# Two-block model on one core: norms by pairs of column blocks, a freed modulation unit, one odd query product among the heads, a joined operand in the first feed-forward

## The chip, the core and the metric

The kernel runs on one core of a Trainium2 chip. The metric is the device time of one execution in microseconds (us). The engines are TensorE (PE in the profile; PEld is its weight load), VectorE (DVE), ScalarE (ACT), GpSimd (POOL) and SyncE (SP), which issues the transfers.

## The reference

A sequence of 256 tokens with 1024 features passes two blocks. The first (linear attention, two softmax attentions, a mixture of 32 experts) fills the first 600 us and is not touched. The second has two layers, each modulated by a condition vector `c`:

```
for l in range(2):
    mod = silu(c) @ ada_w[l] + ada_b[l]          # six parts: shift, scale, gate, twice
    h = rms_norm(x, norm_mix[l]) * (1 + scale1) + shift1
    x = x + gate1 * (mixer[l](h) @ w_out[l])     # layer 0: "even", layer 1: "odd"
    h = rms_norm(x, norm_ffn[l]) * (1 + scale2) + shift2
    x = x + gate2 * ((silu(h @ wg[l]) * (h @ wu[l])) @ wd[l])   # hidden width 2816
```

The odd mixer is attention in a window of 128 tokens: 16 query heads of 64 columns, 4 key heads, a learned sink in the softmax, a bias that falls with distance.

## The kernel before

Everything is in fp32. A product with a weight is made of two parts of each operand: `wh`, the weight cast to fp32r (ScalarE, L344), and `wl`, the rest (VectorE, L346); likewise `xh` and `xl` for the activations (L412, L413). Three products are added up in PSUM: wh·xh, wh·xl, wl·xh. Tokens are two tiles `t` of 128.

Feed-forward: four chunks of hidden columns, two in each half, and behind a half the product with `wd` for it. The gate and up products of layer 0 (`dense_T`, L499 to L501) take the three parts as three passes of 256 columns. Those of layer 1 (`dense_T2`, L480, L481) keep xh and xl side by side in one tile `xx`, so that one pass of 512 columns does wh·xh and wh·xl into two halves of a PSUM bank and one of 256 does wl·xh; the two halves are then added (`ev_g2`, `ev_u2`) by a ScalarE copy and a VectorE add. In layer 0 VectorE also computes eight units of the modulation (L725, L729: one weight piece times a scalar, added up), whose sums over partitions TensorE makes in passes of one column (L747).

Norm: the residual is added in halves of 512 columns, each is squared and summed (`square`, L424), the reciprocal root is made on ScalarE (Ln, Exp; L122) and VectorE, and put on a diagonal (`diag`, L437). A product with `diag` transposes and scales a 128 by 128 block of x (L389: `pt`), and the evacuation applies gain and shift (`evT`, L408 on ScalarE, two of 16 on VectorE, L410) before it is split into xh and xl. Modulation units not on VectorE are eight TensorE passes (`pa`, L719), a copy (`part`, L731) and one or four passes (`pq`, L739) that add up the parts; `MOD_AT` says at which place how many are done: at "ffn0" and "ffn1" two, at "even" and "odd" one.

Odd mixer: after keys and values, `dense` makes the query product of 512 columns for heads 0 to 7 (q0) and 8 to 15 (q1). Each is followed by four blocks of four heads (`Heads`, run by `run_heads`): scores (`ps`, L593), bias and row maximum (L601), Exp (L122), division (L556, L560), transposition (`pT`, L638), product with v (`po`, L648), split into `yh`, `yl`. Blocks of the first token tile have 128 keys, those of the second 256. The order in a queue is chosen when the program is built, by when tiles become free; `after` puts one instruction behind another by hand. `hold` remembers the instructions that others are put behind.

Of the kernel before, what the change touches and what calls it, by code (L numbers as in the profile page):

```python
# [9 lines left out]
F32 = mybir.dt.float32  # L10
# [9 lines left out]
KT = 8  # L20
# [58 lines left out]
def block_kernel(ctx: ExitStack, tc: tile.TileContext, a, out, stop=None):  # L79
# [299 lines left out]
    def to_T(xh, xl, src, t, gain=None, shift=None, pool=None, blocks=(0, 1), tags="tbb", diag=None):  # L379
        last = None  # L380
        for b in blocks:
            turn[1] += 1
            pt = bank("pt", tags[turn[1] % len(tags)])
            for k in range(4):
                piece = src[:, (4 * b + k) * 128:(4 * b + k + 1) * 128]
                if diag is None:
                    PE.transpose(pt[:, 128 * k:128 * k + 128], piece, ident)
                else:
                    i = PE.matmul(pt[:, 128 * k:128 * k + 128], piece, diag, start=True, stop=True)  # L389
                    if k == 0 and hold["pt"]:  # L390
                        after(i, hold["pt"])
                    hold["pt"] = i.ins
# [3 lines left out]
            if gain is None:  # L396
                split(hv, lv, pv)
            else:
                tmp = pool.tile([128, 4, 128], F32, tag="sq", name="evT", bufs=2)
                if shift is None:  # L400
                    V.tensor_tensor(tmp, pv, gain(4 * b, 4)[:, :, None].to_broadcast([128, 4, 128]), ALU.mult)
                    S.copy(hv, tmp)
                    (G if b else V).tensor_sub(lv, tmp, hv)  # L403
                    continue
                g, sh = gain(4 * b, 4), shift(4 * b, 4)
                for k in range(4):
                    if b == 0 or k < 3:
                        i = S.activation(tmp[:, k], pv[:, k], AF.Identity, scale=g[:, k:k + 1], bias=sh[:, k:k + 1])  # L408
                    else:
                        V.tensor_scalar(tmp[:, k], pv[:, k], g[:, k:k + 1], sh[:, k:k + 1], op0=ALU.mult, op1=ALU.add)  # L410
                for h in (slice(0, 2), slice(2, 4)) if b == t == 0 else (slice(0, 4),):
                    V.tensor_copy(hv[:, h], tmp[:, h])  # L412
                    last = (V.tensor_sub(lv[:, h], tmp[:, h], hv[:, h]).ins, i.ins)  # L413
        return last
# [6 lines left out]
    def square(t, c, in_turn=True):  # L421
# [5 lines left out]
        if c:  # L427
            ms = small.tile([128, 1], F32, tag="ms", name="ms")
            V.tensor_tensor(ms, sq[:, t, 0:1], sq[:, t, 1:2], ALU.add)
            norm_parts[1 + t] = rsqrt(ms, 1)  # L430

    def norm_T(xh, xl, gain, shift, pool, place):

        hold["q"], hold["pt"] = [], None
# [3 lines left out]
        for b in range(2):  # L438
            for t in range(2):
                last = to_T(xh, xl, x[:, t], t, gain, shift, pool, blocks=(b,), diag=diag[t])  # L440
                if b == 0:
                    ev0 = last[::-1]

        hold["q"] = [(hold["exp"] if place == "even" else None, hold["diag"]), ev0, last[::-1], last[::-1]]
        hold["last"] = last
# [22 lines left out]
    def dense_T2(xx, name, c0, w, evac, tags):  # L468
# [16 lines left out]

    def dense_T(xh, xl, name, c0, w, evac):

        n = w // 128
        ps = [bank("pd", "d") for _ in range(0, n, 2)]
        for k0 in range(0, KT, 4):  # L490
            wt, = load((name, c0, k0))
            for h0 in (0, 2):
                wh, wl = split_w(wt[:, h0 * w:(h0 + 2) * w])
                for k in range(2):
                    kk = k0 + h0 + k
                    for i in range(n):
                        o = ps[i // 2][:, i % 2 * 256:i % 2 * 256 + 256]
# [1194 lines left out]
```

## Time and profile before

| what | us |
|---|---|
| median of 3 runs (1257.46 to 1259.83) | 1259.74 |
| profiled execution | 1257.98 |
| its span in the trace | 1256.1 |
| first feed-forward (759.88 to 954.36) | 194.48 |
| odd mixer (961.70 to 1058.13) | 96.43 |
| norm ahead of the odd mixer / of the second feed-forward | 7.34 / 10.96 |

The trace counts from the span's start, and 1.88 us of the profiled execution lie outside it. A stage is read as a window: its length, how long each engine was busy in it, and the clock that TensorE was granted.

### The profile page before, as it was taken

Reading aid. Unit: us, or ns where it says so; the run is one execution under the profiler, and the core shown is the slowest. Engines: PE = TensorE matmul, PEld = TensorE weight load, DVE = VectorE, ACT = ScalarE, POOL = GpSimd, SP = SyncE. Lnnn points to the kernel's source line nnn. Section 1 sums busy time; section 2 is a strip of 40 time slices with the busy share of each in tenths; the row PEclk is TensorE's granted clock in tenths of the full one; section 3 lists DMA queues with packets and bytes.
Section 4 is the critical chain, followed back from the end, with each engine's and each line's share of the span. In section 5 each row is a group of like instructions: output and inputs, shape, how many; then the busy total and the mean of one; then the engine's idle time right before and its main releaser. Section 6 shows DMA issues by size and latency. Waiting matters only on the chain.

```text
span 1256.1 us, 17061 instructions
## 1 busy us (share of the span) xinstructions
PE 1153.2 (92%) x6575; PEld 779.5 (62%) x6575; DVE 636.8 (51%) x1403; ACT 473.8 (38%) x999; POOL 17.0 (1%) x23
## 2 busy tenths in 40 slices
PE   8999999789697978787999899999999999999998
PEld 6786764244141414111777559989996766888886
DVE  7687511201010101010689759876856666766674
ACT  5567500000000000000665746443456566664562
POOL 1020000000000000000000000000000000000000
PEclk9999999999998989888999899999999999999999
DMA  9967899999999999999976279978767515656520
GB/s 343 346 210 292 299 389 420 421 420 421 421 421 420 421 421 421 421 421 414 383 287 203 103 246 327 346 255 294 278 213 247 172 34 184 219 188 215 164 72 33
DMA packets 111289, 370.61 MB, mean 295 GB/s; under 512 B 6051, under 2 KB 19174, under 8 KB 86886
## 3 DMA queue, kind: packets, MB, share of 16 engines
q1 hardware_dynamic: 111122, 369.46, 77.7%
q8 instruction: 52, 0.85, 0.3%
q14 instruction: 31, 0.25, 0.1%
q10 hardware_dynamic: 84, 0.04, 0.0%
HBM read 368.43 MB, written 1.05 MB: 294 GB/s over the span
## 4 chain that ended last, share of the span: by engine, by line
PE 58%; DMA 31%; DVE 6%; ACT 3%; issue 0%; SPq 0%; DVEq 0%; ACTq 0%
DMA w<-in_w_gate_dram 10%; DMA w<-in_w_down_dram 10%; DMA w<-in_w_up_dram 9%; PE pd L357 8%; PE pd L361 8%; PE pd L360 8%; PE pd L480 7%; PE pd L499 3%; PE pd L500 3%; PE pd L501 3%; PE pd L481 3%; PE pgx L1442 2%; PE ps L593 2%; DVE wl L346 1%; PE gt L1467 1%; PE pa L719 1%
## 5 line engine op out<-in xcount | busy, mean ns | idle before, releaser
L346 DVE TENSOR_TENSOR wl<-w,wh 128x1024 fp32r<-128x1024 f32 (+5 forms) x264 | 267.8, 1022 | 138.1 <-ACT wh L344 135.1
L344 ACT CAST wh<-w 128x1024 fp32r<-128x1024 f32 (+5 forms) x264 | 231.2, 886 | 221.1 <-PE pd L360 112.3
L1467 PE MATMUL up<-w,xg 128*32 128x512 f32 x512 | 97.4, 682 | 38.8 <-DMA w<-in_w_up_dram 38.8
L480 PE MATMUL pd<-xx,wh 128*128 128x512 f32 x352 | 121.0, 394 | 0.6 <-DVE xx L413 0.6
L1478 DVE TENSOR_TENSOR hm<-hm,up 128x512 f32<-128x512 f32 x8 | 5.5, 688 | 201.6 <-PE up L1467 201.6
L1467 PE MATMUL gt<-w,xg 128*32 128x512 f32 x512 | 87.5, 634 | 20.0 <-DMA w<-in_w_gate_dram 14.3
L1490 PE MATMUL py<-w,hT 128*32 128x512 f32 x512 | 94.2, 609 | 9.6 <-DVE hT L1483 5.5
L499 PE MATMUL pd<-xh,wh 128*128 128x256 f32 x352 | 99.5, 285 | 0.0
L500 PE MATMUL pd<-xl,wh 128*128 128x256 f32 x352 | 99.2, 283 | 0.2 <-DVE xl L413 0.2
L501 PE MATMUL pd<-xh,wl 128*128 128x256 f32 x352 | 98.6, 283 | 0.0
L481 PE MATMUL pd<-xx,wl 128*128 128x256 f32 x352 | 95.3, 278 | 0.0
L357 PE MATMUL pd<-wh,xh 128*128 128x512 f32 (+3 forms) x240 | 90.5, 380 | 0.6 <-ACT wh L344 0.3
L1467 PEld LDWEIGHTS up<-w,xg 128*32 128x32 f32 x512 | 21.6, 121 | 109.1 <-DMA w<-in_w_up_dram 70.4
L360 PE MATMUL pd<-wh,xl 128*128 128x512 f32 (+3 forms) x240 | 88.1, 370 | 0.2 <-DVE xl L403 0.2
L361 PE MATMUL pd<-wl,xh 128*128 128x512 f32 (+3 forms) x240 | 83.7, 379 | 3.1 <-DVE wl L346 2.9
L480 PEld LDWEIGHTS pd<-xx,wh 128*128 128x128 f32 x352 | 65.7, 188 | 16.4 <-DVE xx L413 1.4
L1442 PEld LDWEIGHTS pgx<-hot,xn 128*128 128x128 f32 x256 | 62.4, 333 | 13.6 <-issue 11.6
L357 PE MATMUL pd<-wh,hidh 128*128 128x512 f32 x176 | 68.5, 389 | 0.0
L360 PE MATMUL pd<-wh,hidl 128*128 128x512 f32 x176 | 68.5, 389 | 0.0
L500 PEld LDWEIGHTS pd<-xl,wh 128*128 128x128 f32 x352 | 67.4, 192 | 0.5 <-DVE xl L413 0.4
L499 PEld LDWEIGHTS pd<-xh,wh 128*128 128x128 f32 x352 | 67.2, 192 | 0.8 <-DVE xh L412 0.7
L501 PEld LDWEIGHTS pd<-xh,wl 128*128 128x128 f32 x352 | 67.1, 192 | 0.0
(401 smaller groups left out, 1776.5 us busy)
## 6 DMA issues: line engine op xcount, KB each, us to landing
w<-in_w_gate_dram SPq DMA_DIRECT2D x64, 1024.0 KB, 19.8
w<-in_w_up_dram SPq DMA_DIRECT2D x64, 1024.0 KB, 19.8
w<-in_w_down_dram SPq DMA_DIRECT2D x62, 1024.0 KB, 19.8
w<-in_ada_w_dram SPq DMA_DIRECT2D x48, 1024.0 KB, 5.9
w<-in_ffn_down_dram SPq DMA_DIRECT2D x20, 1024.0 KB, 5.1
w<-in_ffn_gate_dram SPq DMA_DIRECT2D x16, 1024.0 KB, 5.1
w<-in_ffn_up_dram SPq DMA_DIRECT2D x16, 1024.0 KB, 6.2
w<-in_w_out_dram SPq DMA_DIRECT2D x12, 1024.0 KB, 6.4
```

What stands on the lines that cost most here:

```text
L344: i = S.copy(wh[:, :n], src)
L346: j = (G if share[0] and turn[0] % share[0] == 0 else V).tensor_sub(wl[:, :n], src, wh[:, :n])
L357: i = PE.matmul(o, xh, wh, start=start, stop=False)
L360: PE.matmul(o, xl, wh, start=False, stop=False)
L361: hold["pe"] = PE.matmul(o, xh, wl, start=False, stop=stop).ins
L480: PE.matmul(ps[i], wh[:, ws], xx[:, kk], start=kk == 0, stop=kk == KT - 1, skip_group_check=True)
L481: hold["pe"] = PE.matmul(ps[i][:, 0:256], wl[:, ws], xx[:, kk, 0], start=False, stop=kk == KT - 1, skip_group_check=True).ins
L499: PE.matmul(o, wh[:, ws], xh[:, kk], start=kk == 0 and i % 2 == 0, stop=False, skip_group_check=True)
L500: PE.matmul(o, wh[:, ws], xl[:, kk], start=False, stop=False, skip_group_check=True)
L501: hold["pe"] = PE.matmul(o, wl[:, ws], xh[:, kk], start=False, stop=kk == KT - 1, skip_group_check=True).ins
L1467: mm = PE.matmul(o[32 * j:32 * j + 32, :], xg[:, 4 * hk + k, 32 * j:32 * j + 32], ws[j][:, k * 512:(k + 1) * 512], start=hk == 0 and k == ...
L1490: PE.matmul(py[c][32 * j:32 * j + 32, :], hT[:, 2 * hk + k, 32 * j:32 * j + 32], ws[j][k][:, c * 512:(c + 1) * 512], start=hk == 0 and k = ...
```

## The change

- The first feed-forward uses `xx` as the second does; `dense_T` with three passes goes.
- The norm transposes in four PSUM tiles of two column blocks for all 256 tokens; ScalarE evacuates each 128 by 256 piece (8 in all). The passes of the last tile stand behind the first products. EPS is added to the first half's sum early, and Ln takes that sum as its bias, so no add stands between the last square and Ln.
- At "ffn0" and "ffn1" the first of the two units gets no order behind the mixer's last product, its `part` none behind the norm's Exp, and its `pq` none behind the transposes.
- q1 is made in four steps of 12 passes, which stand among the four head blocks of q0. The weight cast of steps 1 to 3 is put behind the last Exp of the softmax before (`hold["soft"]`).

```diff
@@ square
-        if c:
-            ms = small.tile([128, 1], F32, tag="ms", name="ms")
-            V.tensor_tensor(ms, sq[:, t, 0:1], sq[:, t, 1:2], ALU.add)
-            norm_parts[1 + t] = rsqrt(ms, 1)
...
+        elif c == 0:
+            V.tensor_scalar(sq[:, t, 0:1], sq[:, t, 0:1], EPS, None, op0=ALU.add)
+        else:
+            m0, m1 = sq[:, t, 0:1], sq[:, t, 1:2]
...
+            act(y, m1, AF.Ln, bias=m0)
+            hold["exp"] = act(y, y, AF.Exp, scale=-0.5).ins
@@ norm_T
-        for b in range(2):
-            for t in range(2):
-                last = to_T(xh, xl, x[:, t], t, gain, shift, pool, blocks=(b,), diag=diag[t])
...
+        for b, t in ((0, 0), (1, 0), (2, 0), (0, 1), (1, 1), (2, 1), (3, 0), (3, 1)):
+            if t == 0:
+                pts[b] = bank("pt", "tbbb"[b])
+            for k in range(2):
+                at_ = (2 * b + k) * 128
+                i = PE.matmul(pts[b][:, 256 * k + 128 * t:256 * k + 128 * t + 128], x[:, t, at_:at_ + 128], diag[t], start=True, stop=True)
...
+            for k in range(2):
+                i = S.activation(tmp[:, k], pts[b][:, 256 * k:256 * k + 256], AF.Identity, scale=g[:, k:k + 1], bias=sh[:, k:k + 1])
+            for h in (slice(0, 1), slice(1, 2)) if b == 0 else (slice(0, 2),):
...
+                V.tensor_copy(hv, tmp[:, h])
+                j = V.tensor_sub(lv, tmp[:, h], hv)
@@ modulation
+            free = norm and i < n - 1
+            begun.append(ada(*units.pop(0), TAG_AT(place), place in ON_DVE, norm and not free, None, False if free else norm or None))
+            if free or not norm and (len(begun) == 2 or place not in ON_DVE + ('odd1',)):
+                begun.pop(0)()
+        if norm:
+            modulated(hold["pt"])
@@ odd_mixer
+        dense(xh, xl, "odd", *C_ODD[1], ev_q(0))
+        q1 = dense_steps(xh, xl, "odd", *C_ODD[2], ev_q(4))
+
+        def step_q1(i):
+            if i:
+                hold["q"] = [hold["soft"]]
+            next(q1, None)
         for q in range(2):
-            dense(xh, xl, "odd", *C_ODD[1 + q], ev_q(4 * q))
...
+            if q:
+                run_heads(todo, lambda: early({k: (yh[:, k:k + 4], yl[:, k:k + 4]) for k in (0, 4)}))
+            else:
+                run_heads(todo, {i: lambda i=i: step_q1(i) for i in range(4)})
@@ feed-forward
-            if l:
-                xx = p3.tile([128, KT, 2, 256], F32R, tag="xx", name="xx")
-                xh, xl = xx[:, :, 0], xx[:, :, 1]
-            else:
-                xh = p3.tile([128, KT, 256], F32R, tag="xh", name="xh")
-                xl = p3.tile([128, KT, 256], F32R, tag="xl", name="xl")
+            xx = p3.tile([128, KT, 2, 256], F32R, tag="xx", name="xx")
+            xh, xl = xx[:, :, 0], xx[:, :, 1]
...
+                    dense_T(xx, f"ffg{l}", c0, w, ev_g, "dddt")
+                    modulated()
+                    dense_T(xx, f"ffu{l}", c0, w, ev_u, "ssbb")
```

TensorE's queue from the last out-projection product (`pd<-wl,yh`) through the norm ahead of the second feed-forward to its first products; a row with x8 is eight passes of the form. Before:

```order
L361 MATMUL pd<-wl,yh 128x512
L719 MATMUL pa<-w,condr 32x512 x8
L739 MATMUL pq<-part,pick_100 128x512
L719 MATMUL pa<-w,condr 32x512 x8
L389 MATMUL pt<-diag,x 128x128 x16
L739 MATMUL pq<-part,pick_100 128x512
L480 MATMUL pd<-xx,wh 128x512
L481 MATMUL pd<-xx,wl 128x256
```

After the change, behind six passes with the first tile's `diag` that follow the last product:

```order
L728 MATMUL pq<-part,pick_100 128x512
L708 MATMUL pa<-w,condr 32x512 x8
L438 MATMUL pt<-diag,x 128x128 x6
L490 MATMUL pd<-xx,wh 128x512
L491 MATMUL pd<-xx,wl 128x256
L490 MATMUL pd<-xx,wh 128x512
L491 MATMUL pd<-xx,wl 128x256
L490 MATMUL pd<-xx,wh 128x512
L491 MATMUL pd<-xx,wl 128x256
L490 MATMUL pd<-xx,wh 128x512
L491 MATMUL pd<-xx,wl 128x256
L438 MATMUL pt<-diag,x 128x128 x4
```

One unit's eight `pa` passes are gone from here (they stand among the out-projection's products now), the transposes are in pieces of six, six and four, and eight feed-forward products stand ahead of the last four.

TensorE's queue in the odd mixer: before, from the last of q1's products (`pd<-wh,xh` and its like) through the scores of q0's second block (128x128) to those of its wide blocks (128x256).

```order
L357 MATMUL pd<-wh,xh 128x512
L360 MATMUL pd<-wh,xl 128x512
L361 MATMUL pd<-wl,xh 128x512
L593 MATMUL ps<-kT,qT 128x128 x4
L638 MATMUL pT<-ident,sc 128x128 x4
L593 MATMUL ps<-kT,qT 128x256 x4
L648 MATMUL po<-pTs,v 64x128 x4
L357 MATMUL pd<-wh,yh 128x512
L593 MATMUL ps<-kT,qT 128x256 x4
L360 MATMUL pd<-wh,yl 128x512
```

After the change, from the last products of q1's first step, through the scores (`ps`) of the first three blocks, to the products of its second step (the x8 are the scores of two blocks):

```order
L360 MATMUL pd<-wh,xl 128x512
L361 MATMUL pd<-wl,xh 128x512
L556 MATMUL pt<-ident,qn 128x128 x4
L582 MATMUL ps<-kT,qT 128x128 x8
L582 MATMUL ps<-kT,qT 128x256 x4
L627 MATMUL pT<-ident,sc 128x128 x2
L582 MATMUL ps<-kT,qT 128x256 x2
L357 MATMUL pd<-wh,xh 128x512
L360 MATMUL pd<-wh,xl 128x512
L357 MATMUL pd<-wh,xh 128x512
L360 MATMUL pd<-wh,xl 128x512
L627 MATMUL pT<-ident,sc 128x128 x2
```

Before, half of q1's 48 passes stood ahead of the first score block and half between the first and the second, and only the out-projection's products (`pd<-wh,yh`) were left for the later blocks. Now the scores of the first two blocks and of one and a half wide ones follow each other, with one step of q1 ahead and the next behind.

## Rows read from the trace of the kernel before

**Rows 1.** The page: span, and the chain that ended last by engine.

```profile
span 1256.1 us, 17061 instructions
...
PE 58%; DMA 31%; DVE 6%; ACT 3%; issue 0%; SPq 0%; DVEq 0%; ACTq 0%
```

**Rows 2.** Windows by stage: length; PE, PEld, DVE, ACT, POOL busy; clock; DMA share, GB/s.

```profile
602.00:611.00 9.00, 7.43 (x58) 4.98 (x57) 6.25 (x20) 8.58 (x26) 0.00 (x0) 1.00 1.06 378
...
750.00:759.88 9.88, 9.15 (x69) 4.92 (x61) 6.35 (x20) 6.82 (x19) 0.00 (x0) 1.00 0.93 317
759.88:827.47 67.59, 67.37 (x561) 67.10 (x561) 58.46 (x81) 33.03 (x43) 0.00 (x0) 1.00 0.92 324
827.47:857.42 29.95, 29.95 (x135) 24.79 (x133) 26.88 (x36) 12.05 (x13) 0.00 (x0) 1.00 0.85 290
857.42:924.32 66.90, 66.90 (x562) 66.90 (x560) 46.49 (x60) 30.00 (x36) 0.00 (x0) 1.00 0.73 255
...
954.36:961.70 7.34, 6.32 (x52) 4.39 (x51) 5.93 (x21) 6.27 (x18) 0.55 (x2) 1.00 0.59 194
961.70:1058.13 96.43, 91.98 (x493) 66.42 (x491) 66.06 (x201) 62.94 (x172) 0.00 (x0) 0.98 0.40 134
1058.13:1069.09 10.96, 9.58 (x69) 5.07 (x68) 7.36 (x21) 7.58 (x22) 0.00 (x0) 1.00 1.03 373
1069.09:1130.38 61.29, 61.29 (x352) 53.55 (x353) 44.62 (x69) 39.67 (x72) 0.00 (x0) 1.00 0.61 199
...
1160.31:1221.44 61.13, 61.13 (x354) 53.43 (x352) 41.56 (x63) 36.18 (x65) 0.00 (x0) 1.00 0.38 125
```

**Rows 3.** Groups of VectorE, first gate and up half of layer 0 (759.88 to 827.47).

```profile
L729 DVE SCALAR_TENSOR_TENSOR part<-w,condr,part 128x512 f32<-128x512 f32 x28 | 20.0, 745 | 0.0
...
L725 DVE TENSOR_SCALAR part<-w,condr 128x512 f32<-128x512 f32 x4 | 1.8, 480 | 0.0
```

**Rows 4.** Groups of TensorE in the same window.

```profile
L747 PE MATMUL pq<-ones_r,part 128*128 128x1 f32 x32 | 3.8, 240 | 0.0
```

**Rows 5.** Timeline, norm ahead of the second feed-forward.

```profile
1057.34 0.40 PE L357 MATMUL pd<-wh,yh 128*128 128x512 f32 x1
...
1057.57 0.39 PE L360 MATMUL pd<-wh,yl 128*128 128x512 f32 x1
...
1058.13 1.93 PE L719 MATMUL pa<-w,condr 128*32 128x512 f32 x16
...
1060.14 0.59 ACT L731 COPY part<-pa 128x512 f32<-128x512 f32 x1 [0.60 <-DVE ms L429]
...
1061.06 0.61 ACT L424 ACTIVATE sqj<-x 128x512 f32<-128x512 f32 x1
```

**Rows 6.** Windows in the odd heads, columns as in rows 2.

```profile
1003.75:1037.29 33.54, 30.84 (x183) 21.59 (x183) 23.21 (x110) 23.30 (x83) 0.00 (x0) 0.95 0.10 32
1010.00:1015.00 5.00, 4.92 (x19) 3.70 (x17) 3.30 (x17) 3.35 (x16) 0.00 (x0) 0.66 0.44 169
```

**Rows 7.** Groups of ScalarE in the odd mixer.

```profile
L344 ACT CAST wh<-w 128x1024 fp32r<-128x1024 f32 x20 | 20.9, 1051 | 14.4 <-PE pd L360 13.1 <-issue 1.1
L122 ACT ACTIVATE sc<-sc,mx 128x256 f32<-128x256 f32 x16 | 7.9, 498 | 0.0
L122 ACT ACTIVATE sc<-sc,mx 128x128 f32<-128x128 f32 x16 | 6.2, 390 | 3.7 <-DVE mx L605 3.7
...
L556 ACT ACTIVATE sc<-sc,rc 128x256 f32<-128x256 f32 x8 | 3.6, 498 | 0.0
L554 ACT COPY pTs<-pT 128x512 f32<-128x512 f32 x6 | 3.5, 579 | 3.5 <-PE pT L638 3.4
```

**Rows 8.** Groups of TensorE in the odd heads (1003.75 to 1037.29).

```profile
L593 PE MATMUL ps<-kT,qT 64*128 64x256 f32 x32 | 8.6, 402 | 1.1 <-DVE mx L601 1.1
L638 PE MATMUL pT<-ident,sc 128*128 128x128 f32 x32 | 5.1, 283 | 0.0
...
L648 PE MATMUL po<-pTs,v 128*64 128x128 f32 x56 | 4.6, 285 | 0.0
```

More of the change, by code (lines that the diff above doesn't have):

```diff
@@ L377, in rsqrt, with to_T @@
         return y
-    def to_T(xh, xl, src, t, gain=None, shift=None, pool=None, blocks=(0, 1), tags="tbb", diag=None):
-        last = None
+    def to_T(xh, xl, src, t, gain=None, pool=None, blocks=(0, 1), tags="tbb"):
         for b in blocks:
@@ L385, in to_T @@
                 piece = src[:, (4 * b + k) * 128:(4 * b + k + 1) * 128]
-                if diag is None:
-                    PE.transpose(pt[:, 128 * k:128 * k + 128], piece, ident)
-                else:
[L389 to L392, printed above, removed]
+                PE.transpose(pt[:, 128 * k:128 * k + 128], piece, ident)
             hv = xh[:, 4 * b:4 * b + 4, t * 128:(t + 1) * 128]
@@ L399, in to_T @@
                 tmp = pool.tile([128, 4, 128], F32, tag="sq", name="evT", bufs=2)
[L400 to L414, printed above, removed]
+                V.tensor_tensor(tmp, pv, gain(4 * b, 4)[:, :, None].to_broadcast([128, 4, 128]), ALU.mult)
+                S.copy(hv, tmp)
+                (G if b else V).tensor_sub(lv, tmp, hv)
     norm_parts = []
@@ L437, in norm_T @@
             hold["diag"] = V.tensor_scalar(diag[t], ident, norm_parts[1 + t], None, op0=ALU.mult).ins
-        for b in range(2):
-            for t in range(2):
-                last = to_T(xh, xl, x[:, t], t, gain, shift, pool, blocks=(b,), diag=diag[t])
[L441 to L445, printed above, removed]
+        pts, mm = {}, None
+        for b, t in ((0, 0), (1, 0), (2, 0), (0, 1), (1, 1), (2, 1), (3, 0), (3, 1)):
[4 more added lines that the diff above has]
+                i = PE.matmul(pts[b][:, 256 * k + 128 * t:256 * k + 128 * t + 128], x[:, t, at_:at_ + 128], diag[t], start=True, stop=True)
+                if mm:
+                    after(i, mm)
+                mm = i.ins
+        done = []
+        for b in range(4):
+            tmp = pool.tile([128, 2, 256], F32, tag="sq", name="evT", bufs=2)
+            g, sh = gain(2 * b, 2), shift(2 * b, 2)
+            for k in range(2):
+                i = S.activation(tmp[:, k], pts[b][:, 256 * k:256 * k + 256], AF.Identity, scale=g[:, k:k + 1], bias=sh[:, k:k + 1])
+            for h in (slice(0, 1), slice(1, 2)) if b == 0 else (slice(0, 2),):
+                hv, lv = xh[:, 2 * b + h.start:2 * b + h.stop], xl[:, 2 * b + h.start:2 * b + h.stop]
+                V.tensor_copy(hv, tmp[:, h])
+                j = V.tensor_sub(lv, tmp[:, h], hv)
+            done.append((i.ins, j.ins))
+        hold["q"] = [(hold["exp"] if place == "even" else None, hold["diag"]), done[1], done[3], done[3]]
+        hold["pt"], hold["last"] = mm, done[3][::-1]
     def dense(*args, **kw):
@@ L610, in scores @@
                 else:
-                    act(sc[:, h], sc[:, h], AF.Exp, bias=mx[:, h:h + 1], scale=-1.0,
-                                 accum_out=sm[:, h:h + 1])
+                    hold["soft"] = act(sc[:, h], sc[:, h], AF.Exp, bias=mx[:, h:h + 1], scale=-1.0,
+                                       accum_out=sm[:, h:h + 1]).ins, red
             if self.sinks is not None:
@@ L762, in modulation @@
         for i in range(n):
-            begun.append(ada(*units.pop(0), TAG_AT(place), place in ON_DVE, norm, None, i > 0 if norm else None))
-            if len(begun) == 2 or place not in ON_DVE + ('odd1',):
-                begun.pop(0)(hold["pt"] if norm and i == n - 1 else None)
+            free = norm and i < n - 1
[4 more added lines that the diff above has]
+            modulated(hold["pt"])
         if place not in ON_DVE + ('odd1',):
```

63 lines of the change are left out of this document (19 added, 44 removed).

## Prediction

> **What bounds the kernel now.** I read the page first. Its chain names TensorE for 58% and transfers for 31% of the span [rows 1]; the transfers are those of the experts in the first block, which the change does not touch. So I cut the second block into its stages and read each as a window [rows 2]. The reader is to see there that TensorE is busy for all but a few tenths of a microsecond of the feed-forward stages (67.37 of 67.59 us, 66.90 of 66.90, 61.29 of 61.29). In these only fewer or faster passes, or a new wait, change the time. The norms are different: TensorE stands idle for 9.00 - 7.43 = 1.57 us ahead of the even mixer, 9.88 - 9.15 = 0.73 ahead of the first feed-forward, 7.34 - 6.32 = 1.02 ahead of the odd mixer and 10.96 - 9.58 = 1.38 ahead of the second feed-forward, together 4.70. In the odd mixer it is idle for 96.43 - 91.98 = 4.45 us, of which 33.54 - 30.84 = 2.70 lie in the heads [rows 2, 6]. There also lies the one stretch of this mixer with a lower clock: from 1010 to 1015 the mean granted clock is 0.66, a mix of 2.4 and 1.2 GHz, which costs at most 5 x 0.34 = 1.7 us [rows 6]. These are the sums that the parts of the change can draw on.
>
> **The joined operand in the first feed-forward.** Columns streamed are the same (3 x 256 against 512 + 256), passes fall from three to two. The price is in the trace, since the second feed-forward runs the joined form on the same shape, 176 groups in each gate and up half [rows 2]. Its halves took 61.29 and 61.13 us, those of the first 67.59 and 66.90. The difference is 12.07 us, but the halves of the first also hold the column sums of the modulation units, 32 passes with 3.8 us in one half [rows 4] and, by the same number of units' sums, as much in the other. 12.07 - 7.6 = 4.5 us are left for the passes themselves. These 3.8 us are a sum of durations that overlap in the pipeline; if the sums cost only 3.0, the gain is 6.1.
>
> What may take it back is VectorE. In the joined form each tile of 256 columns is added up and multiplied by itself; a half then costs VectorE 44.62 us where it had no modulation to do [rows 2]. The first half of layer 0 has that on top: 28 multiply-adds with 20.0 us and four first products with 1.8 [rows 3]. 44.62 + 21.8 = 66.4 us of work would meet a half of 61.29 + 3.8 = 65.1 us. The `wd` stage behind it has room: VectorE is busy for 26.88 of 29.95 us there [rows 2]. So VectorE goes from a cover that is nearly sufficient to one that is full, and the weight rests `wl`, for which TensorE would wait, stand in its queue among the multiply-adds. The excess of 1.3 us can be pushed into the next stage's 3.1 us of room as far as the order allows; I charge 0.5 us. In the second half 46.49 us now are busy of 66.90, and nothing waits. Term: **-4.0 us**, bounds -6.1 and, if all of the first half's gain is lost in waits and more, -1.0.
>
> The Trainium skill, on the page TensorE: Matmul & The Clock Gate, section Back-to-back issue gap, gives the isolated gap between warm matmuls as columns over 2.4 GHz plus 2.5 ns. By that rule a joined group saves one such 2.5 ns, and 352 groups 0.9 us, as an estimate. This case's windows show 4.5 us for the same step, since the stages differ by more than the rule allows for.
>
> **The norms.** Evacuation goes from 16 pieces of 128 columns to 8 of 256; the add between the last square and Ln goes; the last four passes and one `pq` go behind the first products. None of this takes passes off TensorE, so in sum it can gain no more than the idle time, 4.70 us over the four norms. At the two feed-forwards one unit's eight `pa` passes, 1.93 us [rows 5] (a pass of this kind leaves two records), move into the mixer ahead. Where TensorE is busy there the move is neutral, where it is idle it gains. It also takes a wait out of the chain: before, the copy `part` of 0.59 us at 1060.14 stands on ScalarE ahead of the second tile's square at 1061.06 [rows 5]. What stays is a chain of residual add, square, Ln, Exp, `diag`, evacuation and split, of which no part gets shorter than its instructions. I take somewhat under half of the idle time. Term: **-2.0 us** (-1.2 at the mixers, -0.8 at the feed-forwards), bounds -4.7 and +1.9. The latter is one `pa` group that lands where TensorE is full, while the chain leaves the gap as long as it is.
>
> **q1 among the heads.** Before, the second half of q1 covers only the first score block, and later blocks have out-projection products alone, of which the earliest wait for `yh`. After, steps 1 to 3 of q1 stand between the blocks. A pass of 512 columns takes 1057.57 - 1057.34 = 0.23 us [rows 5], so a step is 12 x 0.23 = 2.8 us. With a wide block's scores (8.6 / 32 x 8 = 2.2), its transpositions (5.1 / 32 x 8 = 1.3) and products with v (4.6 / 56 x 8 = 0.7) [rows 8] TensorE has 7.0 us per wide block. ScalarE has four Exp of 0.498, two divisions of 0.498, a weight cast of 1.05 and a copy of 0.58 [rows 7], 4.6 us. On the whole TensorE stays the bound, and a step of q1 is a better cover than before.
>
> The start is worse. Behind q1's first step come the scores of two narrow blocks and part of a wide one, and the next step's cast is put behind the second block's last Exp. From the first scores that is eight Exp of 0.390 (3.1 us), the cast (1.05), and ahead of them the first block's reductions, about 1 us: some 5.2 us as an estimate from these rows. TensorE has in that time the second block's scores (half of a wide block's 2.2, 1.1) and one and a half wide ones (3.3), 4.4 us, of which the later ones wait for a PSUM bank that the reductions must free first. I charge 1.5 us idle there and 1.0 us at each of the two later casts, 3.5 in all, against 2.70 now. If the clock then stays up, 1.7 are gained. Term: 3.5 - 2.7 - 1.7 = -0.9, rounded to **-1.0 us**. Bounds: -4.4 (no idle, no low clock) and +3.3 (2 us at each of the three casts, 6.0 against 2.7, and the low clock stays as long as it was).
>
> **Sum.** -4.0 - 2.0 - 1.0 = -7.0 us. The profiled execution took 1257.98, so it would become 1251.0. The median of the runs shown is 1.76 higher, 1259.74; taken off that, the forecast is **1252.7 us**.
>
> **Rivals.**
> 1. VectorE becomes the bound of the first feed-forward. For it speaks 66.4 us of work in 65.1; against it the room behind it and 46.49 of 66.90 in the second half [rows 2]. If each of the four units there (21.8 / 4 = 5.5 us) holds TensorE for 1 us, the gain falls by 3.5 more than charged: 1256.2.
> 2. The norms and the heads give nothing, because the moved `pa` passes and the steps of q1 land where TensorE is busy and the chains stay: only -4.0 is left, less 1.9 for one group: 1257.6, near to no change.
> 3. Slower: ScalarE's chain paces q1. If TensorE's waits for the three casts bring the clock to 1.2 GHz, as the heads show it from 1010 to 1015 [rows 6], for as long as the q0 heads last, then q1's 36 passes (8.3 us) and the scores, transpositions and products of two wide blocks (8.4) and two narrow ones (half of that, 4.2) take twice their 20.9 us where they are not waiting anyway. With half of that exposed it is +10.4, and 2.5 more for the waits: -6.0 + 12.9 = +6.9, or 1266.6. It decides from 6 us of low-clock cost on (-6.0 + 2.5 + 6.0 = +2.5). Before, that cost was at most 1.7. The skill's page named above, section Part 1: The HAM clock gate, says that the throttled state is the default and activity releases it; by that rule sparser heads lower the clock, and the trace agrees so far as the clock fell in the heads, where TensorE had just been idle.
> 4. Better: the heads lose all idle time and the low clock (-4.4 in place of -1.0) and the norms three quarters of their idle (-3.5): 1247.8.
> 5. The halves of layer 0 are longer not for their passes alone but for the transfers beside them, whose share was 0.92 and 0.73 where layer 1 had 0.61 and 0.38 [rows 2]. Between the two halves of layer 0, 0.19 of share went with 0.69 us; at that rate the 0.31 and 0.35 between the layers are 2.4 of the 4.5 us, and 2.1 - 0.5 = 1.6 are left: 1255.1. Against it, layer 1's own halves differ by 0.16 us at 0.23 of share.
>
> **How the numbers follow.** Forecast 0.42, rival 1 0.14, rival 2 0.15, rival 3 0.11, rival 4 0.13, rival 5 0.05. What a measurement of this kernel can tell from no change is about 0.2%, 2.5 us. Faster by more than that: forecast, rivals 4 and 5, and, since it lies just beyond, a little over half of rival 1, together 0.68. Within it: rival 2 and part of what is left of rival 1, 0.20. Slower: rival 3, 0.12 with the far end of rival 1. The range reaches down to rival 4 and up past no change, from 1247 to 1260.5 us; what it leaves out is rival 3 and a gain beyond rival 4.
>
> **What would show it.** In the profile after, the gate and up halves of layer 0 should last about 65 us with TensorE busy throughout; waits of its passes for `wl` there would show rival 1. The gap ahead of the second feed-forward should fall from 10.96 to some 8.6 us, since 1.93 us of passes leave it, with those passes found in the odd heads. In the heads TensorE's waits should stand at the weight casts behind Exp, and the granted clock in them at or near 1.00; a clock under 0.8 over 10 us or more would show rival 3. The forecast is wrong if VectorE, not TensorE, ends the first feed-forward's stages, or if the odd mixer grows by more than 2 us beyond the `pa` passes that it takes in.

## The result and the profile after

The changed kernel takes 1266.58 us (median of 5 runs, 1264.4 to 1267.32) against 1259.74 (5 runs); the ratio is 1.0055, interval 1.0044 to 1.0066. It is slower by 0.55%, where 0.56% faster was forecast. The page of the changed kernel has:

```profile
span 1264.7 us, 16480 instructions
...
PE 1157.3 (92%) x6223; PEld 760.5 (60%) x6223; DVE 648.3 (51%) x1459; ACT 484.6 (38%) x1039; POOL 16.9 (1%) x23
...
PE 19%; DVE 3%; ACT 1%; issue 0%; DVEq 0%; ACTq 0%
```

The span grew by 8.6 us in the profiled execution. It is cut below at the stages' ends, as [rows 2]: the windows of the changed kernel, with length, busy time of PE, PEld, DVE, ACT and POOL, granted clock, DMA share and GB/s.

```profile
752.46:764.85 12.39, 8.90 (x44) 5.00 (x43) 5.63 (x16) 4.93 (x16) 0.00 (x0) 0.72 0.44 153
764.85:832.54 67.69, 67.57 (x395) 58.76 (x395) 64.32 (x113) 40.62 (x74) 0.00 (x0) 1.00 0.84 292
862.52:927.55 65.03, 65.03 (x385) 57.26 (x384) 53.42 (x91) 36.32 (x65) 0.00 (x0) 1.00 0.77 274
963.49:1064.84 101.35, 92.48 (x516) 65.48 (x516) 68.03 (x203) 64.29 (x172) 0.00 (x0) 1.00 0.45 151
1064.84:1075.97 11.13, 7.63 (x43) 4.16 (x43) 5.64 (x16) 4.88 (x15) 0.00 (x0) 0.85 0.38 121
```

They are the norm ahead of the first feed-forward (now 12.39 us with a mean clock of 0.72), its first gate and up half (with the norm's last passes in it, 1.3 us), its second half, the odd mixer, and the norm ahead of the second feed-forward (11.13 us, clock 0.85). From the same marks in both traces:

| from, to | before | after | difference |
|---|---|---|---|
| even norm and mixer (first `diag` pass to last product) | 143.52 | 145.85 | +2.33 |
| that product to the first gate product | 10.27 | 12.39 | +2.12 |
| first gate and up half, layer 0 | 67.59 | 67.69 | +0.10 |
| second half | 66.90 | 65.03 | -1.87 |
| its end, over `wd` and norm, to the odd mixer's first product | 37.38 | 35.93 | -1.45 |
| odd mixer, first to last product | 96.33 | 101.35 | +5.02 |
| that product to the second feed-forward's first | 11.05 | 11.13 | +0.08 |
| its first half | 61.29 | 62.97 | +1.68 |

These make 8.0 us; 0.5 us more lie ahead of the even norm, in the part that the change leaves alone. Gains are in two places, the second half and the norm ahead of the odd mixer. The last row's 1.68 us are passes that left the norm: four transposes and one `pq` now stand in that half. The timeline of the changed kernel at the first feed-forward's norm shows the largest new thing:

```profile
752.22 0.40 PE L361 MATMUL pd<-wl,yb 128*128 128x512 f32 x1
...
755.21 0.29 DVE L431 TENSOR_SCALAR diag<-ident,ry 128x128 f32<-128x128 f32 x1
...
755.46 0.56 ACT L720 COPY part<-pa 128x512 f32<-128x512 f32 x1
...
755.55 2.93 PE L438 MATMUL pt<-diag,x 128*128 128x128 f32 x12 [2.94 <-DVE diag L431]
...
757.00 0.29 DVE L431 TENSOR_SCALAR diag<-ident,ry 128x128 f32<-128x128 f32 x1
...
758.28 1.91 PE L728 MATMUL pq<-part,pick 128*128 128x512 f32 x2
...
760.12 2.64 PE L708 MATMUL pa<-w,condr 128*32 128x512 f32 x16
...
762.69 1.60 PE L438 MATMUL pt<-diag,x 128*128 128x128 f32 x12
...
764.85 0.50 PE L490 MATMUL pd<-xx,wh 128*128 128x512 f32 x1 [0.55 <-DVE xx L451]
```

Behind the last product, at 752.22, TensorE waits 2.94 us for the first `diag`. Before, the freed unit's eight passes stood there. Then the first transposes, `pq` and the greater part of `pa` run at 1.2 GHz: 12 records of transposes take 2.93 us where the next 12 take 1.60, `pq` takes 1.91 us for what is 1.02 at 2.4 GHz, `pa` 2.64 for 1.92. The second tile's `diag` is there at 757.29, but its transposes wait in the queue behind `pq` and `pa` until 762.69.

### The profile page after: what moved, and what is told of

It reads as the page before. It is cut to its first block, busy times and chain, and to the rows that moved or that the text cites. A ratio compares the mean times of both kernels' runs of the same rounds, so it can differ in the third digit from the quotient of the medians.

```text
span 1264.7 us, 16480 instructions
## 1 busy us (share of the span) xinstructions
PE 1157.3 (92%) x6223; PEld 760.5 (60%) x6223; DVE 648.3 (51%) x1459; ACT 484.6 (38%) x1039; POOL 16.9 (1%) x23
## 5 line engine op out<-in xcount | busy, mean ns | idle before, releaser
L490 PE MATMUL pd<-xx,wh 128*128 128x512 f32 x704 | 241.4, 396 | 1.2 <-DVE xx L451 1.1
L491 PE MATMUL pd<-xx,wl 128*128 128x256 f32 x704 | 186.5, 279 | 0.0
L490 PEld LDWEIGHTS pd<-xx,wh 128*128 128x128 f32 x704 | 130.2, 188 | 30.7 <-DVE xx L451 1.5
L491 PEld LDWEIGHTS pd<-xx,wl 128*128 128x128 f32 x704 | 130.0, 188 | 2.8 <-issue 0.5
L1490 PE MATMUL py<-w,hT 128*32 128x512 f32 x512 | 100.4, 623 | 10.3 <-DVE hT L1483 5.5
L1467 PE MATMUL gt<-w,xg 128*32 128x512 f32 x512 | 82.6, 602 | 18.6 <-DMA w<-in_w_gate_dram 12.9
L1490 PEld LDWEIGHTS py<-w,hT 128*32 128x32 f32 x512 | 24.7, 111 | 67.3 <-issue 44.9
L1442 PE MATMUL pgx<-hot,xn 128*128 128x128 f32 x256 | 64.8, 408 | 0.0
L1467 PEld LDWEIGHTS gt<-w,xg 128*32 128x32 f32 x512 | 18.3, 109 | 70.2 <-issue 42.4
L361 PE MATMUL pd<-wl,hidh 128*128 128x512 f32 x176 | 60.2, 389 | 0.0
```

The costliest lines, as they stand in the source:

```text
L361: hold["pe"] = PE.matmul(o, xh, wl, start=False, stop=stop).ins
L490: PE.matmul(ps[i], wh[:, ws], xx[:, kk], start=kk == 0, stop=kk == KT - 1, skip_group_check=True)
L491: hold["pe"] = PE.matmul(ps[i][:, 0:256], wl[:, ws], xx[:, kk, 0], start=False, stop=kk == KT - 1, skip_group_check=True).ins
L1442: mm = PE.matmul(pgx[:, k * 128:(k + 1) * 128], xn[:, t, k0 + k::8], hot[:, t].rearrange("p e s -> p (e s)"), start=t == 0, stop=t == 1)
L1467: mm = PE.matmul(o[32 * j:32 * j + 32, :], xg[:, 4 * hk + k, 32 * j:32 * j + 32], ws[j][:, k * 512:(k + 1) * 512], start=hk == 0 and k == ...
L1490: PE.matmul(py[c][32 * j:32 * j + 32, :], hT[:, 2 * hk + k, 32 * j:32 * j + 32], ws[j][k][:, c * 512:(c + 1) * 512], start=hk == 0 and k = ...
```

## Experiments

Each run is compared with the kernel before, timed beside it, whose medians were 1258.37 to 1259.71 us. Names are those of the runs.

**The four parts alone.** The first takes `dense_T2` for layer 0 and nothing else:

```diff
-            if l:
-                xx = p3.tile([128, KT, 2, 256], F32R, tag="xx", name="xx")
+            xx = p3.tile([128, KT, 2, 256], F32R, tag="xx", name="xx")
...
+                    dense_T(xx, f"ffg{l}", c0, w, ev_g, "dddt")
```

> The kernel before with the joined operand in the first feed-forward alone. Theory A (the loss sits at the norms and in the odd heads; the joined operand gains what the two profiles show between the ends of the first feed-forward's stages, 67.59 to 66.35 and 66.90 to 65.03 us): 3.1 us faster, 1256.6. Theory B (the joined operand is itself dear, because VectorE's extra adds hold up the units and their successors): no gain, 1259.7 or more.

The second takes the new `square` and `norm_T`:

```diff
+        for b, t in ((0, 0), (1, 0), (2, 0), (0, 1), (1, 1), (2, 1), (3, 0), (3, 1)):
...
+            act(y, m1, AF.Ln, bias=m0)
```

> The kernel before with the norms by pairs of column blocks alone; both modulation units stay tied to the last product. Theory A (what hurts at the norms is TensorE left without work, which the tied unit's passes prevent): between 2 us faster and no change, 1257.7 to 1259.7, with the granted clock at 1.00 at the feed-forwards' norms. Theory B (the order of the pairs is what hurts, since the second unit's passes stand between the transposes): 3 to 5 us slower, 1263 to 1265.

The third frees the first unit:

```diff
+            free = norm and i < n - 1
+            begun.append(ada(*units.pop(0), TAG_AT(place), place in ON_DVE, norm and not free, None, False if free else norm or None))
```

> The kernel before with the first unit's passes freed from the last product alone. Theory A: TensorE has no work for 3 to 4 us behind the last product at both feed-forwards, the clock falls to 1.2 GHz behind it, and the time is 3 to 6 us longer, 1263 to 1266. Theory B (the order of the pairs hurts): the freed passes are only moved, 0 to 1 us, about 1260.

The fourth puts q1 among the heads:

```diff
+                run_heads(todo, {i: lambda i=i: step_q1(i) for i in range(4)})
```

> The kernel before with the second odd query product among the heads alone. Theory A (q1's steps wait for the casts behind Exp): the odd mixer is 101.35 us against 96.43 with 1.93 of it from the freed unit's passes and 1.3 from the norm's last passes, so 1.6 us slower, 1261.3. Theory B (that growth is the norm's and the freed unit's doing alone): no change or up to 1 us faster, 1258.7 to 1259.7.

| run | median us | ratio | interval |
|---|---|---|---|
| j_only | 1257.66 | 0.9994 | 0.9985 to 1.0003 |
| n_only | 1257.97 | 1.0001 | 0.9992 to 1.0010 |
| f_only | 1266.28 | 1.0057 | 1.0043 to 1.0071 |
| q_only | 1264.09 | 1.0037 | 1.0023 to 1.0050 |

The order of the pairs does not hurt by itself, so that rival fell. The freed unit alone loses as much as the whole change, 7.9 us between the medians (0.57% by the ratio, 7.2 us), more than either theory said; q1 among the heads loses 5.7 (0.37%, 4.7 us), also more. The joined operand's two halves are these (j_only, columns as above):

```profile
762.93:829.61 66.68, 66.35 (x384) 57.43 (x385) 63.43 (x111) 39.52 (x74) 0.00 (x0) 1.00 0.85 303
859.54:924.57 65.03, 65.03 (x385) 57.30 (x384) 54.50 (x93) 36.32 (x65) 0.00 (x0) 1.00 0.78 276
```

The second is 65.03 us as in the changed kernel. The first gains 0.91, but the gap ahead of it grows from 10.27 to 10.98, since the first joined pass needs `xl` as well as `xh`. Timed, little is left of it. The timeline of f_only at the second feed-forward's norm is the most telling:

```profile
1066.54 0.40 PE L361 MATMUL pd<-wl,yh 128*128 128x512 f32 x1
...
1068.89 0.59 ACT L731 COPY part<-pa 128x512 f32<-128x512 f32 x1 [0.32 <-DVE ms L429]
...
1069.62 1.10 PE L739 MATMUL pq<-part,pick 128*128 128x512 f32 x2 [2.68 <-ACT part L731]
...
1069.81 0.61 ACT L424 ACTIVATE sqj<-x 128x512 f32<-128x512 f32 x1
...
1070.64 1.92 PE L719 MATMUL pa<-w,condr 128*32 128x512 f32 x16
...
1071.81 0.29 DVE L437 TENSOR_SCALAR diag<-ident,ry 128x128 f32<-128x128 f32 x1
...
1072.50 3.92 PE L389 MATMUL pt<-diag,x 128*128 128x128 f32 x32
...
1077.85 0.50 PE L480 MATMUL pd<-xx,wh 128*128 128x512 f32 x1 [0.57 <-DVE xx L413]
```

The first unit's passes are not in this gap, and the gap is not shorter: 11.07 us against 11.05. TensorE waits 2.68 us for the copy `part`, makes `pq`, and only then the second unit's `pa`, which stands behind `pq` in the queue. The kernel before has at the same place:

```profile
1057.80 0.40 PE L361 MATMUL pd<-wl,yh 128*128 128x512 f32 x1
...
1063.06 0.29 DVE L437 TENSOR_SCALAR diag<-ident,ry 128x128 f32<-128x128 f32 x1
...
1063.75 3.91 PE L389 MATMUL pt<-diag,x 128*128 128x128 f32 x32
```

The chain from the last product to the second tile's `diag` takes 1071.81 - 1066.54 = 5.27 us without the first unit's passes and took 1063.06 - 1057.80 = 5.26 with them, and the transposes start 0.40 us behind that `diag` in both. The copy `part` also still stands ahead of the second tile's square on ScalarE (1068.89 and 1069.81). The passes are paid in the mixers instead: the even mixer grew by 1.96 us (140.37 to 142.33 from first to last product), the odd one by 2.99 (96.33 to 99.32).

At the first feed-forward the gap of f_only even grew, from 10.27 us to 11.90:

```profile
756.63 1.46 PE L739 MATMUL pq<-part,pick 128*128 128x512 f32 x2 [2.57 <-ACT part L731]
758.01 3.23 PE L719 MATMUL pa<-w,condr 128*32 128x512 f32 x16
```

Here `pa` takes 3.23 us, for the most part at 1.2 GHz (a stretch of 3.4 us from 757.3 on), behind a wait of 2.57 us; at the second feed-forward it takes 1.92 behind a wait of 2.68. So a wait of this length brings the low clock in one place and not in the other, and what decides was not found. The two mixers, this gap and 0.88 us in the second feed-forward's first half (see the last section) make 7.5 us.

**The passes left out.** The freed unit's passes are not made at all, in the kernel before and in f_only:

```diff
-                if not on_dve:
+                if drop:
+                    pass
+                elif not on_dve:
...
-        if not on_dve:
+        if drop:
+            G.tensor_copy(part, wt[:, 0:512])
+        elif not on_dve:
```

> The kernel before, but the first modulation unit at each of the two feed-forward norms is left out of TensorE's work (its eight passes are not made; a copy of raw weights by GpSimd stands for their sum, so these two modulation vectors are wrong). Theory A (in the gap behind the last product the chain through diag sets the time and the unit's 1.93 us there are free): no change, 1258.4, or up to 1.5 us slower because TensorE idles and its clock falls. Theory B (TensorE is what fills the gap): 3.9 us faster, 1254.5.

> The kernel before with the first unit freed, and that unit's passes left out in the same way (same two vectors wrong). Theory A (the freed passes cost their full 1.93 us in each mixer, since TensorE is the bound there): some 4 us less than the freed kernel's 1266.3, 1262.4; what is left over the kernel before is the idle gap and the low clock. Theory B (the passes themselves cost little, the waits that they bring along and the clock cost it all): within 1 us of 1266.3.

b_drop: 1263.41 us, ratio 1.0032 (1.0020 to 1.0044). f_drop: 1262.37, ratio 1.0020 (1.0011 to 1.0029). Both fit theory A, the first beyond its number: with 3.9 us less work the kernel is 4 us slower. f_drop is 0.37%, 4.7 us, faster than f_only (1.0057), but that is not the price of the passes alone. In the two traces f_drop's mixers are 6.27 us shorter (142.91 for 145.32 from the even norm's first `diag` pass on, 95.46 for 99.32), with 3.4 us less at 1.2 GHz in each, and its gaps are 3.50 longer (12.39 for 11.90, 14.08 for 11.07). That its time meets theory A's number is a balance of the two. b_drop's norm ahead of the second feed-forward, DVE and TensorE:

```profile
1058.85 0.39 PE L361 MATMUL pd<-wl,yh 128*128 128x512 f32 x1
...
1062.46 0.28 DVE L437 TENSOR_SCALAR diag<-ident,ry 128x128 f32<-128x128 f32 x1
...
1062.88 2.05 PE L389 MATMUL pt<-diag,x 128*128 128x128 f32 x8 [3.65 <-DVE rv L370]
...
1063.64 0.29 DVE L437 TENSOR_SCALAR diag<-ident,ry 128x128 f32<-128x128 f32 x1
...
1064.73 1.92 PE L743 MATMUL pq<-part,pick 128*128 128x512 f32 x2
...
1066.57 2.81 PE L721 MATMUL pa<-w,condr 128*32 128x512 f32 x16
```

TensorE waits 3.65 us for `diag`, and what follows is at 1.2 GHz: 2.05 us for eight records that took 1.16 at this place of the odd norm in the kernel before, 1.92 for two `pq` passes, 2.81 for `pa`. The gap is 14.18 us against 11.05. The queue has another order too: `pq` and `pa` stand behind the first four transposes here, and ahead of all sixteen in the kernel before. So this run alone does not tell the clock from the order. A GpSimd copy stands for the ScalarE copy here; it is done at 1061.96, ahead of the first `diag`.

**Work for nobody in the gap.** The changed kernel with passes whose result nobody reads:

```diff
                 pts[b] = bank("pt", "tbbb"[b])
+            if b == t == 0 and place in ("ffn0", "ffn1"):
+                for n in range(24):
+                    mm = PE.transpose(pts[0][:, 0:128], ident, ident).ins
```

> The changed kernel with 24 transpositions of the identity into the first PSUM tile of the norm, right behind the last product of both mixers (work for nobody; the results are unchanged). Theory A (TensorE's idle 2.94 us there brings the clock to 1.2 GHz, and pq, pa and the transposes then cost up to twice their time): the clock stays at 2.4 GHz in both gaps, the gap of the first feed-forward falls from 12.4 to about 10 us and that of the second from 11.1 to about 10, together 3 us faster than the changed kernel, 1263.5 to 1264. Theory B (the gap is set by the order of the queue whatever the clock): within 0.5 us of the changed kernel, 1266.6, or longer by what the 24 passes delay.

1263.71 us, ratio 1.0034 (1.0020 to 1.0047) where the changed kernel has 1.0055: 24 useless passes at two places make it some 2.7 us faster. The same place as in the timeline of the changed kernel:

```profile
750.63 0.39 PE L361 MATMUL pd<-wl,yb 128*128 128x512 f32 x1
750.86 2.78 PE L438 MATMUL pt<-ident 128*128 128x128 f32 x24
753.96 1.60 PE L443 MATMUL pt<-diag,x 128*128 128x128 f32 x12 [0.32 <-DVE diag L431]
755.41 1.02 PE L733 MATMUL pq<-part,pick 128*128 128x512 f32 x2
756.36 1.92 PE L713 MATMUL pa<-w,condr 128*32 128x512 f32 x16
758.21 1.60 PE L443 MATMUL pt<-diag,x 128*128 128x128 f32 x12
760.37 0.50 PE L495 MATMUL pd<-xx,wh 128*128 128x512 f32 x1 [0.55 <-DVE xx L456]
```

All is at 2.4 GHz: `pq` 1.02, `pa` 1.92. From the last product to the first gate product it is 9.50 us in place of 12.39, at the second feed-forward 9.53 in place of 11.13. Theory A holds; so what these gaps last beyond 9.5 us in the changed kernel, 2.9 and 1.6 us, is the low clock. The order of the queue is the same in both. The 0.34% that a_fill still loses is not in the gaps.

**The changed kernel with both units tied**, all but the third part:

```diff
-            free = norm and i < n - 1
+            begun.append(ada(*units.pop(0), TAG_AT(place), place in ON_DVE, norm, None, i > 0 if norm else None))
```

> The changed kernel with both units tied to the last product again. Theory A (the freed unit costs what it costs alone, 7 us or so, and the other parts add up: joined -0.7, norms 0, q1 +5.7): 1263.4 against 1266.6 for the changed kernel, since together with the norms' pairs the freed unit costs less than alone. Theory B (the parts are independent): 1266.6 - 7.9 = 1258.7.

1262.41 us, ratio 1.0024 (1.0014 to 1.0034): nearer to theory A. In company the freed unit costs 0.31%, 3.9 us, where it costs 0.57%, 7.2 us, alone.

**Two gains together**: the first and second part, without the others.

> The kernel before with the joined operand and the norms by pairs, without the freed unit and with q1 ahead of the heads as before. Theory A (the two parts that cost nothing alone add up): 0.7 us faster than the kernel before, within 1.5. Theory B (the joined operand, which needs both parts of the normed input at once, gets them earlier from the pairs): 2 to 3 us faster than the kernel before.

1255.13 us, ratio 0.9970 (0.9960 to 0.9981), 0.30% or 3.8 us: beyond theory A and theory B, and faster than both kernels. The changed kernel is this one with q1 among the heads (no_f, 0.54% more) and the freed unit (0.31% more): -0.30 + 0.54 + 0.31 = 0.55. In company q1 is the dearer of the two. The cause that theory B names was not tested by itself. The two windows of its first feed-forward's norm and of its odd mixer:

```profile
749.24:758.75 9.51, 7.87 (x59) 3.89 (x59) 5.63 (x16) 4.86 (x15) 0.00 (x0) 1.00 0.96 310
957.68:1054.79 97.11, 91.51 (x500) 65.57 (x500) 67.53 (x203) 64.00 (x172) 0.00 (x0) 1.00 0.40 136
```

With both units in the gap and the pairs, TensorE is not left alone for long and the clock stays at 1.00; the gap is 9.51 us, and q1's old order has no low clock this time. Norm and first half make 77.16 us, 77.66 with the joined operand alone, 77.86 before.

**q1 among the heads.** In q_only the waits of TensorE from 985 us on (line waited for: us, times, longest), and the odd mixer's window:

```profile
PE ps L593 <- DVE mx L601: 3.1, 5, 0.9
PE pd L361 <- DVE wl L346: 1.4, 2, 0.9
PE pt L567 <- DVE ru L374: 1.3, 1, 1.3
```

```profile
963.26:1063.49 100.23, 91.81 (x492) 65.93 (x490) 66.80 (x200) 62.70 (x172) 0.00 (x0) 0.97 0.38 129
```

In the kernel before the first kind is 1.1 us; in the changed kernel it is 3.1, where the casts hold TensorE up for 0.8:

```profile
PE ps L593 <- DVE mx L601: 1.1, 3, 0.5
```

```profile
PE ps L582 <- DVE mx L590: 3.1, 5, 0.9
PE pt L556 <- DVE ru L374: 1.3, 1, 1.3
PE pd L357 <- ACT wh L344: 0.8, 1, 0.8
```

So it is the scores that wait, for row maxima. First test: only the last two casts are held back.

```diff
-            if i:
+            if i > 1:
                 hold["q"] = [hold["soft"]]
```

> The kernel before with q1 among the heads, but only the casts of steps 2 and 3 are put behind an Exp; steps 0 and 1 may go ahead of the heads (without any such order the queue of TensorE is that of the kernel before). Theory A (the loss comes from scores that follow each other with nothing between them, so it stays while two steps are held back): 2 to 4 us over the kernel before, 1260.4 to 1262.4, with waits of the scores for the row maxima. Theory B (the loss is the first step's cast alone, which comes too late): the loss of 5.7 us goes, 1258.4.

1263.88 us, ratio 1.0030 (1.0019 to 1.0041), with 13.7 us at 1.2 GHz from 1000.9 on. The time is theory A's, at the upper end, so the loss does not go when the second step is free. The scores still wait 2.2 us for row maxima; but the stretch at 1.2 GHz is twice q_only's 6.8, and this run does not tell what is waits and what is clock. Then each cast is put one block earlier, so that steps and score blocks alternate:

```diff
+                    if h == 0:
+                        hold["soft_prev"] = hold.get("soft")
...
-                hold["q"] = [hold["soft"]]
+                hold["q"] = [hold["soft_prev"]]
```

> The kernel before with q1 among the heads, but each cast is put behind the Exp of the block before the one that it waited for, so that a step of q1 stands between the second and the third score block. Theory A (the loss comes from scores that follow each other: each waits until the row maxima of the one before have freed its PSUM banks): most of the 5.7 us of q1 among the heads goes, 1259 to 1261 beside 1259.4, and the waits of scores for row maxima fall from 3.1 us to 1.5 or less. Theory B (any order in which q1 is not done ahead of the heads loses, because its own heads start later): 3 to 6 us over the kernel before, 1262.4 to 1265.4.

> The joined operand and the norms by pairs, both units tied, and q1 among the heads with each cast one block earlier. Theory A: within 1.5 us of the kernel without q1 among the heads, 1255.1, either way. Theory B: 3 to 7 us more than that, 1258 to 1262.

q_prev: 1263.26 us, ratio 1.0025 (1.0015 to 1.0035). jn_qprev: 1257.47, ratio 0.9987 (0.9978 to 0.9995). The same two views of q_prev:

```profile
PE pd L357 <- ACT wh L344: 1.4, 2, 0.8
PE pt L567 <- DVE ru L374: 1.3, 1, 1.3
PE pd L361 <- DVE wl L346: 0.9, 1, 0.9
PE ps L593 <- DVE mx L601: 0.9, 2, 0.6
```

```profile
961.50:1059.10 97.60, 89.93 (x497) 63.59 (x499) 67.10 (x201) 62.11 (x171) 0.00 (x0) 1.00 0.40 132
```

The scores' wait for row maxima is 0.9 us, the clock 1.00, and the mixer 97.60 us where q_only has 100.23. So the view shows theory A's cause removed, and q_only's 6.8 us at 1.2 GHz with it, and in this profiled execution (1259.13 us) the time is that of the kernel before. But it is the shortest of twelve, of which seven took 1262.7 to 1264.4 us. The median keeps 0.25%, which is theory B's lower end, and the interval overlaps that of q_only (1.0023 to 1.0050). What the longer executions do in the heads was not profiled. Beside the two gains the earlier cast takes most of the loss away: no_f to jn is 0.54%, jn_qprev to jn 0.17%. Between no_f and jn_qprev the scores' waits for row maxima fall from 3.1 to 1.5 us, and 10.2 us at 1.2 GHz in the odd mixer go; the two are not told apart.

**Passes for nobody in the even heads**, ahead of the stretch at 1.2 GHz that the kernel before has there (693.6 to 703.8):

```diff
+                if fill:
+                    junk = bank("junk", "d")
+                    for n in range(fill):
+                        mm = PE.transpose(junk[:, 0:128], ident, ident)
```

> The kernel before with the joined operand, and with 40 transpositions of the identity into a PSUM tile that nobody reads, in the 4.7 us in which TensorE waits in the even heads ahead of a stretch of 10.2 us at 1.2 GHz. Theory A (idle TensorE lowers the clock, and what follows pays for it): the stretch is gone or shorter, the even mixer is 2 to 3 us shorter than its 140.4, and the time is about 1255 to 1256 beside 1258.4 to 1259.7 for the kernel before, better than both kernels. Theory B (the chain through VectorE sets the time there whatever the clock): no change against the joined operand alone, 1257.7 to 1259.

> The joined operand, the norms by pairs, and the 40 transpositions for nobody in the even heads. Theory A (the gains have separate places, so they add: norms and joined operand -0.30%, the passes in the even heads -0.25%): 0.5% under the kernel before, 1253 beside 1259.4, with the even mixer near 137.5 us and at most one stretch of 3.4 us at 1.2 GHz in it. Theory B (with the pairs alone the stretch at 1.2 GHz in the even heads was already 6.8 us in place of 10.2, so most of the gain is the same one): within 1 us of the kernel without the passes, 1255.1.

j_fill: 1255.53 us, ratio 0.9969 (0.9960 to 0.9978), theory A's time: the stretch is 3.4 us instead of j_only's 10.2, the even mixer 138.71 us instead of 140.47. These 1.76 us are a little less than theory A said, and not all of the 0.25% between j_only and j_fill; in the two traces the odd mixer differs by as much (97.30 and 95.32), where the passes are not. jn_fill: 1256.93, ratio 0.9976 (0.9964 to 0.9988), theory B: the even mixer is 138.67 with 3.4 us at 1.2 GHz and was 138.69 in jn with 6.8. So the passes do not add to jn; of the versions run, jn and j_fill are the fastest.

## Why the prediction was wrong

Over jn, no_f and the changed kernel the runs give -3.8 us for the joined operand and the pairs, +6.8 for q1 among the heads and +3.9 for the freed unit, +6.9 in all. The terms were -4.0 for the operand, -2.0 for pairs and unit and -1.0 for q1.

**The step that failed** first is in the norms: "Where TensorE is busy there the move is neutral, where it is idle it gains." I took the passes in the gap as work that the gap must hold, so that the gap would shrink by 1.93 us when they left, to "some 8.6 us". They lay beside a chain that sets the gap, and were free there. f_only shows the gap of the second feed-forward unchanged at 11.07 us, with the second `diag` 5.27 us behind the last product as before (5.26), while the mixers pay 1.96 and 2.99 us. My bound for this term, +1.9, was one group of passes; two are paid, and they cost more than their 3.9 us. Nor did freeing the unit alone take the copy `part` from ahead of the second tile's square, as I had said.

**What I left out** is the clock in the gap. The prediction speaks of the clock in the odd heads alone. Taking TensorE's only work out of the first 3 us of a gap left it idle for 2.94 us, and the work behind then ran at 1.2 GHz; b_drop and a_fill show it from both sides, less work being slower and useless work faster. In the changed kernel the low clock is 2.9 and 1.6 us of the two gaps, and filling them gives back 0.21% of the 0.55. The Trainium skill, on the page TensorE: Matmul & The Clock Gate, in Part 1: The HAM clock gate, says that the throttled state is the default and activity releases it; the runs agree for the most part (the changed kernel's windows are at 0.72 and 0.85 without passes there, a_fill's passes run at 2.4 GHz), but in f_only's second gap the passes behind a wait of 2.68 us still ran at 2.4 GHz. I had put that rule to the heads and not to the place from which the change takes work.

**q1 among the heads**: the place was right ("the start is worse"), the size wrong: forecast -1.0, measured +3.9 us in q_only's odd mixer (96.33 to 100.23) and 0.37% in time. In company it is the greatest loss, 0.54%. I charged 3.5 us of idle in place of 2.70, 0.8 more; TensorE is idle for 100.23 - 91.81 = 8.42 us against 4.45 before [rows 2], 4.0 more. Of these 1.6 lie ahead of the second group's first scores, and 2.4 behind them, in the second group and the out-projection, for which I charged nothing. I looked for the waits at the casts; for the greater part they stand at the scores, which wait for the row maxima that free their PSUM banks; these I had named but priced only within the 1.5 us at the start. The sign that I had named came: the changed kernel's odd mixer grew by 5.02 us, 3.1 more than the `pa` passes that it takes in. The 1.7 us of low clock that I counted as won were won there, where the clock is 1.00; in q_only the stretch doubled instead, from 3.4 to 6.8 us. q_prev shows that the scores' waits come from the order of the casts; what remains of its 0.25% stays open.

**The joined operand** was right in kind and half in size: forecast -4.0, in j_only's trace -2.1. The second half is as forecast, 1.87 us gained for 66.90 - 61.13 - 3.8 = 2.0. The first gains 0.91 where 2.5 less 0.5 was forecast, and 0.71 go back in the gap ahead of it, since the first joined pass needs `xl` too, which I had not counted. VectorE, busy for 63.43 of that half's 66.68 us, held TensorE up for 0.8 us at its start and at one column sum and not for the weights' rests, so rival 1 fell; the rest of the first half's shortfall lies where TensorE is busy (66.35 of 66.68 us), and its cause stays open. Timed alone, the part is within the noise (0.9994).

**The norms by pairs** alone give nothing measurable (1.0001). What they take from a gap comes back in the stage behind it, which holds the last four transposes: from j_only to jn the gap of the second feed-forward falls from 11.06 to 9.52 us and the half behind it grows from 61.29 to 62.97. At the first, gap and half together gain 0.5 us, and the odd norm falls from 7.42 to 6.32. I had forecast -0.8 for the two, the freed unit included. Beside the joined operand the pairs seem worth 0.24%. Part of that is where the stretches at 1.2 GHz happened to lie, and how much was not settled.

**Rivals**: rival 3 named the low clock as the way to a slower kernel, at +12.9 us in the heads. Its 1266.6 meets the measured 1266.58 by luck: its sign, a clock under 0.8 over 10 us in the heads, did not come, and the changed kernel's odd mixer ran at 1.00. The low clock came at the norms, for 0.21% of the 0.55. Rival 2, with moved passes landing where TensorE is busy, named the freed unit's half of it: it counted 1.9 us for one group.

## What to carry to other kernels

Before moving work out of a gap, ask what the gap's length comes from: passes beside a longer chain are free there and may cost in full elsewhere. Ask also what TensorE will do in the time that becomes empty, because the work behind an empty stretch may run at 1.2 GHz, as it did here behind 2.57, 2.94 and 3.65 us and did not behind 2.68. Where steps share PSUM banks, put work that could cover their waits between them and don't hold it back behind them: one block earlier was worth 0.37% here (no_f to jn_qprev).

## What the runs showed unexpectedly

Leaving out 3.9 us of TensorE's work made the kernel 4 us slower (b_drop, 1.0032), and 48 passes for nobody made the changed kernel 0.21% faster (a_fill). The odd mixer with the same queue took 96.3 us with 3.4 us at 1.2 GHz (the kernel before) and 97.3 with 6.8 (j_only), so some 1 us of any comparison of these kernels is where such a stretch falls. The first half of the second feed-forward, whose code is the same in the kernels without the pairs, took 61.29 us in some kernels (the one before, j_only) and 62.17 in others (f_only, q_only) with TensorE busy throughout and a clock of 1.00; around 1091 us a group of a joined and a single pass comes every 0.353 us in f_only and every 0.346 in the kernel before. Why is not known; these 0.9 us are part of what f_only and q_only lose.
